# Loops in place of unrolled VectorE and ScalarE programs in a streamed LoRA-style matrix product

## The chip, the cores and the metric

One core of one Trainium2 chip. The metric is device microseconds of one execution, the median of several runs.

## The reference

```python
x_flat = x.reshape(-1, in_dim)            # 32768 x 256, fp32
y = x_flat @ W                            # W 256 x 256
lora_out = x_flat @ lora_A                # 256 x 16
lora_out = lora_out * lora_E              # 16
lora_out = lora_out @ lora_B              # 16 x 256
y = y + scale * lora_out                  # scale 1.0
return y.reshape(batch, seq_len, out_dim) # fp32
```

## The kernel before, in words

The kernel folds the low-rank branch into one weight: weff = W + (lora_A scaled by lora_E) @ lora_B, in bf16, made once at the start (lines 166 to 184). Then it streams x through: 33.5 MB in, 33.5 MB out.

The 32768 rows are cut by PLAN into five blocks of 56, 56, 48, 48 and 48 rows per partition. Three buffers of those sizes (SLOTS) hold blocks 0, 1 and 2; blocks 3 and 4 reuse the first two once the stores that read them have landed. Loads are cut into pieces (PIECES), each with a semaphore of its own; a store is one transfer for a whole block. The result of a row overwrites x in the same buffer. All loads of x, W and all stores are issued by SyncE (SP), so they run on one queue, in the order load 0, 1, 2, store 0, store 1, load 3, load 4, store 2, 3, 4. The three small matrices lora_A, lora_B and lora_E are issued by ScalarE on its own queue.

Computing goes in 32 steps of S = 8 rows per partition. In each step

- VectorE casts 8 rows to bf16 (`rounded`, L159, tile xb),
- TensorE transposes them, two bf16 values at a time packed as one fp32 word (`transposed`, L198, psum_xt),
- VectorE copies the transposed tile to SBUF (`copied`, L163, tile xt),
- TensorE multiplies by weff (`multiplied`, L209, psum_y), in two halves of G = 4 rows,
- ScalarE copies each half back into the block's buffer (L232, tile xy).

Everything is double-buffered by step parity. TensorE's program is already a loop (`Fori`) of two steps a turn, in the order transposes of step t+1, matmuls of step t. The programs of VectorE and ScalarE are written out step by step: each instruction waits for a semaphore to reach a count.

VectorE's order is rounded(0), rounded(1), then copied(t), rounded(t+2) for t = 0 to 31. At step 16 (HOLD) it stops until store 0 has landed and then makes five casts of 128x4096 into a tile nobody reads (L157); that is the pause that the title of the change speaks of. ISSUE_LOAD, ISSUE_STORE and ISSUE_PRODUCTS hold back certain issues of SyncE until so many transposes or products are done.

Of the kernel before, what the change touches and what calls it, by code (L numbers as in the profile page):

```python
# [4 lines left out]
PLAN = [56, 56, 48, 48, 48]  # L5

PIECES = {0: [16, 16, 24], 1: [16, 16, 24], 2: [24, 24], 3: [24, 24], 4: [24, 24]}

SLOTS = [56, 56, 48]
LEAD = 3  # L10
AFTER = {1: [3, 4]}

HOLD = 16, 0, 5


ISSUE_LOAD, ISSUE_STORE = {4: 20}, {3: 29}
ISSUE_PRODUCTS = {1: 30}

S, G = 8, 4
P = 128  # L20
FP32 = mybir.dt.float32
BF16 = mybir.dt.bfloat16
# [15 lines left out]
def kernel(tc, x, W, lora_A, lora_B, lora_E, scale, out):  # L38
    nc = tc.nc
    x_flat = x.flatten_outer_dims()  # L40
    out_flat = out.flatten_outer_dims()
    N, K = x_flat.shape
    M = out_flat.shape[1]
    R = lora_B.shape[0]
# [4 lines left out]
    steps = [(i, r) for i, b in enumerate(PLAN) for r in range(0, b, S)]  # L49
    NS = len(steps)  # L50
    assert NS % 2 == 0

    def rows_of(flat, i):
        b, r0 = PLAN[i], starts[i]
        return flat[r0:r0 + b * P, :].rearrange("(p b) k -> p b k", b=b)

    def sbuf(name, shape, dt):
        return nc.alloc_sbuf_tensor(name, shape, dt).ap()

    def psum(name, shape, dt):  # L60
        return nc.alloc_psum_tensor(name, shape, dt).ap()

    slots = [sbuf(f"xy{s}", [P, rows, K], FP32) for s, rows in enumerate(SLOTS)]
    a_sb = sbuf("a_sb", [P, KC, R], FP32)
    e_sb = sbuf("e_sb", [R, 1], FP32)
    w_sb = sbuf("w_sb", [P, KC, M], FP32)
    b_sb = sbuf("b_sb", [R, M], FP32)
    b_bf = sbuf("b_bf", [R, M], BF16)
    ate = sbuf("ate", [R, KC, P], BF16)
    weff = sbuf("weff", [P, KC, M], BF16)  # L70
    spare = sbuf("spare", [P, 2 * S, K], BF16)
    ident = sbuf("ident", [P, P], FP32)

    xb = [sbuf(f"xb{k}", [P, S, K], BF16) for k in range(2)]
    words = [t[:, :, :].rearrange("p s k -> p (s k)").bitcast(FP32).rearrange("p (s w) -> p s w", s=S) for t in xb]

    xt = [sbuf(f"xt{k}", [P, S, P], FP32) for k in range(2)]
    pairs = [t[:, :, :].rearrange("p s t -> p (s t)").bitcast(BF16).rearrange("p (s t c) -> p s t c", s=S, c=KC) for t in xt]
    ps_xt = [psum(f"psum_xt{k}", [P, S, P], FP32) for k in range(2)]
    ps_y = [psum(f"psum_y{k}", [P, G, M], FP32) for k in range(2)]  # L80
# [4 lines left out]
    s_w, s_a, s_b, s_e = (Count(nc, f"s_{k}") for k in "wabe")  # L85

    pieces = {}
    for i, b in enumerate(PLAN):
        parts = PIECES.get(i, [b])
        pieces[i] = [(sum(parts[:j]), n) for j, n in enumerate(parts)]  # L90
    s_ld = {(i, r): Count(nc, f"s_ld{i}_{r}") for i in pieces for r, n in pieces[i]}
    s_st = [Count(nc, f"s_st{i}") for i in range(len(PLAN))]
    s_id, s_set, s_v, s_t, s_m, s_y = (
        Count(nc, k) for k in ("s_id", "s_set", "s_v", "s_t", "s_m", "s_y"))
    tick = nc.alloc_semaphore("tick")


    can_m = nc.alloc_semaphore("can_m")
    can_t = [nc.alloc_semaphore(f"can_t{k}") for k in range(2)]
    can_y = [[nc.alloc_semaphore(f"can_y{h}_{k}") for k in range(2)] for h in range(S // G)]  # L100

    def slot(i):
        return slots[i % LEAD][:, :PLAN[i], :]

    opening = []

    def transfer(queue, count, **aps):
        ins = queue.dma_start(**aps)
        for names in opening:
            names.add(ins.ins.name)  # L110
        count.by(ins, 16)

    def load(i):
        for r, n in pieces[i]:
            transfer(nc.sync, s_ld[i, r], out=slot(i)[:, r:r + n, :], in_=rows_of(x_flat, i)[:, r:r + n, :])

    def store(i):
        transfer(nc.sync, s_st[i], out=rows_of(out_flat, i), in_=slot(i))

    def spent(engine, count):  # L120
        engine.wait_ge(count.sem, count.total).then_inc(count.sem, -count.total)

    def take(sem):
        nc.tensor.wait_ge(sem, 1).then_inc(sem, -1)
# [4 lines left out]
    transfer(nc.sync, s_w, out=w_sb, in_=W.rearrange("(p c) m -> p c m", c=KC))  # L129
    transfer(nc.scalar, s_a, out=a_sb, in_=lora_A.rearrange("(p c) r -> p c r", c=KC))  # L130
    transfer(nc.scalar, s_b, out=b_sb, in_=lora_B)
    transfer(nc.scalar, s_e, out=e_sb, in_=lora_E[:, None])
    load(0)
    opening.clear()
    tc.close()
# [1 line left out]
    for i in range(1, LEAD):  # L137
# [5 lines left out]
        out=ident, in_=ident, compare_op=mybir.AluOpType.not_equal, fill=1.0, base=0,  # L143
        pattern=[[-1, P]], channel_multiplier=1))


    def rounded(t):
        i, r = steps[t]
        if (i, r) in s_ld:
            nc.vector.wait_ge(s_ld[i, r].sem, 16)  # L150
        if t == HOLD[0]:

            for _ in range(10):
                nc.vector.engine_nop()
            nc.vector.wait_ge(s_st[HOLD[1]].sem, 16)
            for _ in range(HOLD[2]):
                nc.vector.tensor_copy(out=spare, in_=slot(i)[:, r:r + 2 * S, :]).then_inc(tick, 1)  # L157
                nc.vector.wait_ge(tick, 1).then_inc(tick, -1)
        nc.vector.tensor_copy(out=xb[t % 2], in_=slot(i)[:, r:r + S, :]).then_inc(can_t[t % 2], 1)  # L159

    def copied(t):
        nc.vector.wait_ge(s_t.sem, t + 1)
        nc.vector.tensor_copy(out=xt[t % 2], in_=ps_xt[t % 2]).then_inc(can_m, 1)  # L163


    nc.vector.wait_ge(s_b.sem, 16)
    s_v.by(nc.vector.tensor_copy(out=b_bf, in_=b_sb))  # L167
    nc.tensor.wait_ge(s_a.sem, 16)
    nc.tensor.wait_ge(s_id.sem, 2)
    for c in range(KC):  # L170
# [4 lines left out]
    s_v.by(nc.vector.tensor_scalar(  # L175
        out=ate, in0=ps_at, scalar1=e_sb, scalar2=float(scale),
        op0=mybir.AluOpType.mult, op1=mybir.AluOpType.mult))
    nc.tensor.wait_ge(s_v.sem, 2)
    for c in range(KC):
        aeb_done = nc.tensor.matmul(ps_aeb[:, c, :], ate[:, c, :], b_bf, start=True, stop=True)  # L180
    s_set.by(aeb_done)
    nc.vector.wait_ge(s_w.sem, 16)
    nc.vector.wait_ge(s_set.sem, 2)
    s_v.by(nc.vector.tensor_add(out=weff, in0=w_sb, in1=ps_aeb))  # L184
    rounded(0)
    rounded(1)
    for t in range(NS):
        copied(t)
        if t + 2 < NS:
            rounded(t + 2)  # L190

    nc.vector.sem_inc(can_t[NS % 2], 1)


    def transposed(k):
        nc.tensor.wait_ge(can_t[k], 1)
        for j in range(S):
            done = nc.tensor.transpose(ps_xt[k][:, j, :], words[k][:, j, :], ident)  # L198
            if j == 1:
                done.then_inc(can_t[k], -1)  # L200
        done.then_inc(s_t.sem, 1)

    def multiplied(k):
        take(can_m)
        for h in range(S // G):
            nc.tensor.wait_ge(can_y[h][k], 1)
            for j in range(G):
                for c in range(KC):
                    done = nc.tensor.matmul(  # L209
                        ps_y[h][:, j, :], pairs[k][:, h * G + j, :, c], weff[:, c, :],  # L210
                        start=(c == 0), stop=(c == KC - 1))
                if j == 0:
                    done.then_inc(can_y[h][k], -1)
            done.then_inc(s_m.sem, 1)

    transposed(0)
    nc.tensor.wait_ge(s_v.sem, 3)

    with nc.tensor.Fori(0, NS // 2):
        for k in range(2):  # L220
            transposed(1 - k)
            multiplied(k)
    s_t.total, s_m.total = NS + 1, NS * S // G

    for h in range(S // G):
        nc.scalar.sem_inc(can_y[h][0], 1)
    n = 0
    for i, r in [(i, r + g) for i, r in steps for g in range(0, S, G)]:
        n += 1
        nc.scalar.wait_ge(s_m.sem, n)  # L230
        t, h = divmod(n - 1, S // G)
        y = nc.scalar.copy(out=slot(i)[:, r:r + G, :], in_=ps_y[h])  # L232
        free = can_y[h][(t + 1) % 2]
        if r + G < PLAN[i]:
            y.then_inc(free, 1)
        else:
            done = s_y.by(y)
            if n < s_m.total:
                nc.scalar.wait_ge(s_y.sem, done)
                nc.scalar.sem_inc(free, 1)  # L240
            nc.sync.wait_ge(s_y.sem, done)
            if i in ISSUE_STORE:
                nc.sync.wait_ge(s_t.sem, ISSUE_STORE[i])
            if i in ISSUE_PRODUCTS:
                nc.sync.wait_ge(s_m.sem, ISSUE_PRODUCTS[i])
            store(i)
            for later in AFTER.get(i, []):
                nc.sync.wait_ge(s_st[later - LEAD].sem, 16)
                if later in ISSUE_LOAD:
                    nc.sync.wait_ge(s_t.sem, ISSUE_LOAD[later])  # L250
                load(later)


    for count in [s_a, s_id]:
        spent(nc.tensor, count)
    spent(nc.tensor, s_v)
    for count in [s_b, s_e, s_w, s_set] + list(s_ld.values()):
        spent(nc.vector, count)
    spent(nc.scalar, s_m)
    nc.tensor.wait_ge(can_y[0][NS % 2], 1).then_inc(can_y[0][NS % 2], -1)  # L260
    for count in [s_y, s_t] + s_st:
        spent(nc.sync, count)


# [33 lines left out]
```

## Time and profile before

| what | us |
|---|---|
| median of 3 runs (161.62 to 162.06) | 161.67 |
| the profiled execution's own time | 161.75 |
| its span, from the first instruction to the last | 160.4 |
| TensorE busy, matmuls | 91.8 (57%) |
| VectorE busy | 87.9 (55%) |
| ScalarE busy | 63.2 (39%) |
| GpSimd busy | 0.7 |
| 64 copies of ScalarE, L232, 1017 ns each | 61.9 |
| 512 matmuls, L209, 280 ns each | 63.7 |
| 264 transposes, L198, 287 ns each | 36.8 |
| 32 copies xt, L163, 1222 ns each | 39.1 |
| 32 casts xb, L159, 1220 ns each | 38.9 |
| 5 casts of the pause, L157, 2294 ns each | 11.5 |

Engines: PE is TensorE, PEld its weight loads, DVE VectorE, ACT ScalarE, POOL GpSimd, SP SyncE; SPq is SyncE's issue of transfers. The row of digits of an engine or of DMA cuts the span into 40 slices, each digit a busy share in tenths. DMA is the mean over the core's 16 DMA engines. Rows of stretches give, for each stretch of the span, its length, busy time and number of instructions of PE, PEld, DVE, ACT and POOL, the TensorE clock granted, the DMA share and the GB/s moved; packets are counted where they begin, so a share can pass 1. Rows of the timeline give start, duration, engine, line, operation and count. q1 is SyncE's queue, q10 ScalarE's, q14 the fetching of instructions.

### The profile page before, as it was taken

Reading aid. Unit: us, or ns where it says so; the run is one execution under the profiler, and the core shown is the slowest. Engines: PE = TensorE matmul, PEld = TensorE weight load, DVE = VectorE, ACT = ScalarE, POOL = GpSimd, SP = SyncE. Lnnn points to the kernel's source line nnn. Section 1 sums busy time; section 2 is a strip of 40 time slices with the busy share of each in tenths; the row PEclk is TensorE's granted clock in tenths of the full one; section 3 lists DMA queues with packets and bytes.
Section 4 is the critical chain, followed back from the end, with each engine's and each line's share of the span. In section 5 each row is a group of like instructions: output and inputs, shape, how many; then the busy total and the mean of one; then the engine's idle time right before and its main releaser. Section 6 shows DMA issues by size and latency. Waiting matters only on the chain. (4 is left out here: it accounts for less than half of the span.)

```text
span 160.4 us, 1883 instructions
## 1 busy us (share of the span) xinstructions
PE 91.8 (57%) x780; PEld 82.7 (52%) x780; DVE 87.9 (55%) x72; ACT 63.2 (39%) x65; POOL 0.7 (0%) x6
## 2 busy tenths in 40 slices
PE   0149999999999600000009999999999960000000
PEld 0028889999999500000008999999999950000000
DVE  0187769998988000039999669899898500000000
ACT  1100675868676700000001768686868670000000
POOL 1000000000000000000000000000000000000000
PEclk9999999999999975555555999999999999555555
DMA  5999999999999999999989999999999999999994
GB/s 179 409 433 447 429 415 433 449 435 411 466 404 392 458 457 457 457 443 457 415 386 382 423 404 460 411 455 423 496 404 404 466 453 429 404 417 490 429 429 196
DMA packets 2802, 67.42 MB, mean 420 GB/s; under 512 B 480, under 2 KB 496, under 8 KB 624
## 3 DMA queue, kind: packets, MB, share of 16 engines
q1 hardware_dynamic: 2592, 67.37, 98.0%
q10 hardware_dynamic: 208, 0.03, 0.2%
q14 instruction: 2, 0.02, 0.0%
HBM read 33.85 MB, written 33.55 MB: 420 GB/s over the span
## 5 line engine op out<-in xcount | busy, mean ns | idle before, releaser
L232 ACT COPY xy<-psum_y 128x1024 f32<-128x1024 f32 x64 | 61.9, 1017 | 65.5 <-PE psum_y L209 65.5
L209 PE MATMUL psum_y<-weff,xt 128*128 128x256 bf16 x512 | 63.7, 280 | 0.1
L209 PEld LDWEIGHTS psum_y<-weff,xt 128*128 128x128 bf16 x512 | 51.4, 101 | 7.1 <-issue 0.3
L198 PE MATMUL psum_xt<-ident,xb 128*128 128x128 f32 x264 | 36.8, 287 | 31.3 <-DVE xb L159 31.3
L198 PEld LDWEIGHTS psum_xt<-ident,xb 128*128 128x128 f32 x264 | 31.9, 148 | 32.7 <-DVE xb L159 32.3
L163 DVE COPY xt<-psum_xt 128x1024 f32<-128x1024 f32 x32 | 39.1, 1222 | 8.4 <-PE psum_xt L198 8.2
L159 DVE CAST xb<-xy 128x2048 bf16<-128x2048 f32 x32 | 38.9, 1220 | 3.7 <-DMA xy<-in_x_dram 3.4
L157 DVE CAST spare<-xy 128x4096 bf16<-128x4096 f32 x5 | 11.5, 2294 | 19.5 <-DMA out_dram<-xy 19.0
L167 DVE CAST b_bf<-b_sb 16x256 bf16<-16x256 f32 x1 | 0.3, 281 | 5.6 <-DMA b_sb<-in_lora_B_dram 5.6
L171 PE MATMUL psum_xt<-ident,a_sb 128*16 128x128 f32 x2 | 0.6, 396 | 4.2 <-POOL ident L142 4.2
L232 ACT ACT_TABLE_LOAD x1 | 1.3, 1283 | 3.5 <-PEq L136 3.5
L180 PE MATMUL psum_xt<-b_bf,ate 16*128 16x256 bf16 x2 | 0.6, 404 | 3.6 <-DVE ate L175 3.6
L171 PEld LDWEIGHTS psum_xt<-ident,a_sb 128*16 128x16 f32 x2 | 0.1, 90 | 4.2 <-DMA a_sb<-in_lora_A_dram 4.2
L180 PEld LDWEIGHTS psum_xt<-b_bf,ate 16*128 16x128 bf16 x2 | 0.1, 106 | 4.1 <-DVE ate L175 4.1
L175 DVE TENSOR_SCALAR ate<-psum_xt,e_sb 16x256 bf16<-16x256 f32 x1 | 0.5, 472 | 2.0 <-DMA e_sb<-in_lora_E_dram 2.0
L184 DVE TENSOR_TENSOR weff<-w_sb,psum_xt 128x512 bf16<-128x512 f32 x1 | 0.7, 689 | 0.8 <-PE psum_xt L180 0.8
L142 POOL TENSOR_SCALAR_AFFINE_SELECT ident<-ident 128x128 f32<-128x128 f32 x1 | 0.3, 294 | 0.2 <-POOL ident L140 0.2
L140 POOL MEMSET ident<- 128x128 f32 x1 | 0.2, 205 | 2.9 <-POOLq L136 2.9
L279 POOL MEMSET const-bfloat16-1.0<- 128x1 bf16 x1 | 0.1, 102 | 0.0
L279 POOL MEMSET const-uint8-127<- 128x1 uint8 x1 | 0.1, 102 | 0.0
L279 POOL MEMSET const-float32-0.0<- 128x1 f32 x1 | 0.1, 99 | 0.2 <-issue 0.2
L279 POOL MEMSET const-float32-1.0<- 128x1 f32 x1 | 0.1, 99 | 0.0
## 6 DMA issues: line engine op xcount, KB each, us to landing
xy<-in_x_dram SPq DMA_DIRECT2D x8, 3072.0 KB, 27.9
out_dram<-xy SPq DMA_DIRECT2D x3, 6144.0 KB, 28.2
out_dram<-xy SPq DMA_DIRECT2D x2, 7168.0 KB, 34.3
xy<-in_x_dram SPq DMA_DIRECT2D x4, 2048.0 KB, 17.8
w_sb<-in_W_dram SPq DMA_DIRECT2D x1, 256.0 KB, 3.0
a_sb<-in_lora_A_dram ACTq DMA_DIRECT2D x1, 16.0 KB, 3.1
b_sb<-in_lora_B_dram ACTq DMA_DIRECT2D x1, 16.0 KB, 4.4
e_sb<-in_lora_E_dram ACTq DMA_DIRECT2D x1, 0.1 KB, 6.2
```

Source lines behind the costliest of these rows:

```text
L142: s_id.by(nc.gpsimd.affine_select(out=ident, in_=ident, compare_op=mybir.AluOpType.not_equal, fill=1.0, base=0, pattern=[[-1, P]], channel ...
L157: nc.vector.tensor_copy(out=spare, in_=slot(i)[:, r:r + 2 * S, :]).then_inc(tick, 1)
L159: nc.vector.tensor_copy(out=xb[t % 2], in_=slot(i)[:, r:r + S, :]).then_inc(can_t[t % 2], 1)
L163: nc.vector.tensor_copy(out=xt[t % 2], in_=ps_xt[t % 2]).then_inc(can_m, 1)
L171: at_done = nc.tensor.transpose(ps_at[:, c, :], a_sb[:, c, :], ident)
L175: s_v.by(nc.vector.tensor_scalar(out=ate, in0=ps_at, scalar1=e_sb, scalar2=float(scale), op0=mybir.AluOpType.mult, op1=mybir.AluOpType.mult))
L180: aeb_done = nc.tensor.matmul(ps_aeb[:, c, :], ate[:, c, :], b_bf, start=True, stop=True)
L184: s_v.by(nc.vector.tensor_add(out=weff, in0=w_sb, in1=ps_aeb))
L198: done = nc.tensor.transpose(ps_xt[k][:, j, :], words[k][:, j, :], ident)
L209: done = nc.tensor.matmul(ps_y[h][:, j, :], pairs[k][:, h * G + j, :, c], weff[:, c, :], start=(c == 0), stop=(c == KC - 1))
L232: y = nc.scalar.copy(out=slot(i)[:, r:r + G, :], in_=ps_y[h])
L279: nc = _bacc.Bacc("TRN2", target_bir_lowering=False, num_devices=1)
```

## The change

- The three buffers become one tensor, xy, of RING = 160 rows; the blocks start in it at AT = 0, 56, 112, 0, 48.
- VectorE's program becomes two casts and two loops of two steps a turn (9 turns, then 7), ScalarE's two loops of two steps a turn (10, then 6). The row in the ring comes from the loop's register. Semaphores are counted down by the waiting instruction, so that each turn waits for the same value. The last copy of a turn signals through last_y, which ScalarE itself waits for before it frees the PSUM half and counts s_y, now once per two steps.
- GpSimd waits for each piece of x and adds its number of steps to s_rows; VectorE's casts wait for s_rows. The pause is on GpSimd, ahead of the piece that starts at step 17: it waits for store 0 and makes seven memsets of a 128x2048 fp32 tile, one after the other.
- SyncE's conditions for stores and loads are counts of s_y (turns).
- lora_E is issued by SyncE between W and the first piece of x. ScalarE copies it to a tile of its own (e_copy) before its loops.
- TensorE makes one matmul whose result nobody reads ahead of the product of lora_A and lora_B, and two behind it (`idle`).

```diff
-SLOTS = [56, 56, 48]
+RING, AT = 160, [0, 56, 112, 0, 48]
-HOLD = 16, 0, 5
-ISSUE_LOAD, ISSUE_STORE = {4: 20}, {3: 29}
-ISSUE_PRODUCTS = {1: 30}
+HOLD = 17, 0, 7
+ISSUE_LOAD, ISSUE_STORE = {4: 9}, {1: 8, 3: 14}
...
-    transfer(nc.scalar, s_e, out=e_sb, in_=lora_E[:, None])
+    transfer(nc.sync, s_e, out=e_sb, in_=lora_E[:, None])
...
+    t = 0
+    for i, r in s_ld:
+        n = sum(rows for first, rows in pieces[i] if first == r) // S
         if t == HOLD[0]:
-            for _ in range(10):
-                nc.vector.engine_nop()
-            nc.vector.wait_ge(s_st[HOLD[1]].sem, 16)
+            nc.gpsimd.wait_ge(s_st[HOLD[1]].sem, 16)
             for _ in range(HOLD[2]):
-                nc.vector.tensor_copy(out=spare, in_=slot(i)[:, r:r + 2 * S, :]).then_inc(tick, 1)
-                nc.vector.wait_ge(tick, 1).then_inc(tick, -1)
+                tick.by(nc.gpsimd.memset(spare, 0.0))
+                nc.gpsimd.wait_ge(tick.sem, tick.total)
+        nc.gpsimd.wait_ge(s_ld[i, r].sem, 16).then_inc(s_rows, n if t + n < NS else n + 2)
+        t += n
+
+    def idle(times):
+        for _ in range(times):
+            nc.tensor.matmul(ps_y[0][:, :2, :].rearrange("p g m -> p (g m)"), ident, w_sb[:, :, :].rearrange("p c m -> p (c m)"),
+                             start=True, stop=True)
...
+    nc.tensor.wait_ge(s_w.sem, 16)
+    idle(1)
     nc.tensor.wait_ge(s_v.sem, 2)
...
     s_set.by(aeb_done)
+    idle(2)
...
+    def rounded(k, first):
+        nc.vector.wait_ge(s_rows, 1).then_inc(s_rows, -1)
+        nc.vector.tensor_copy(out=xb[k], in_=xy[:, bass.ds(first, S), :]).then_inc(can_t[k], 1)
+
+    for k in range(2):
+        rounded(k, k * S)
+    around = RING // (2 * S) - 1
+    for turns, begin in ((around, 2 * S), (NS // 2 - around, 0)):
+        with nc.vector.Fori(0, turns) as turn:
+            for k in range(2):
+                nc.vector.wait_ge(s_t, 1).then_inc(s_t, -1)
+                nc.vector.tensor_copy(out=xt[k], in_=ps_xt[k]).then_inc(can_m, 1)
+                rounded(k, turn * (2 * S) + (begin + k * S))
...
+    nc.scalar.wait_ge(s_e.sem, 16)
+    nc.scalar.copy(out=e_copy, in_=e_sb)
...
+    for turns in (RING // (2 * S), NS // 2 - RING // (2 * S)):
+        with nc.scalar.Fori(0, turns) as turn:
+            for k in range(2):
+                for h in range(S // G):
+                    nc.scalar.wait_ge(s_m, 1).then_inc(s_m, -1)
+                    first = turn * (2 * S) + (k * S + h * G)
+                    y = nc.scalar.copy(out=xy[:, bass.ds(first, G), :], in_=ps_y[h])
+                    y.then_inc(can_y[h][1] if k == 0 else can_y[0][0] if h == 0 else last_y, 1)
+            nc.scalar.wait_ge(last_y, 1).then_inc(last_y, -1)
+            nc.scalar.sem_inc(can_y[1][0], 1)
+            nc.scalar.sem_inc(s_y.sem, 1)
+    s_y.total = NS // 2
+    rows = 0
+    for i, b in enumerate(PLAN):
+        rows += b
+        nc.sync.wait_ge(s_y.sem, -(-rows // (2 * S)))
+        if i in ISSUE_STORE:
+            nc.sync.wait_ge(s_y.sem, ISSUE_STORE[i])
+        store(i)
+        for later in AFTER.get(i, []):
+            nc.sync.wait_ge(s_st[later - LEAD].sem, 16)
+            if later in ISSUE_LOAD:
+                nc.sync.wait_ge(s_y.sem, ISSUE_LOAD[later])
+            load(later)
```

More of the change, by code (lines that the diff above doesn't have):

```diff
@@ L61, in psum @@
         return nc.alloc_psum_tensor(name, shape, dt).ap()
-    slots = [sbuf(f"xy{s}", [P, rows, K], FP32) for s, rows in enumerate(SLOTS)]
+    xy = sbuf("xy", [P, RING, K], FP32)
     a_sb = sbuf("a_sb", [P, KC, R], FP32)
     e_sb = sbuf("e_sb", [R, 1], FP32)
+    e_copy = sbuf("e_copy", [R, 1], FP32)
     w_sb = sbuf("w_sb", [P, KC, M], FP32)
@@ L70 @@
     weff = sbuf("weff", [P, KC, M], BF16)
-    spare = sbuf("spare", [P, 2 * S, K], BF16)
+    spare = sbuf("spare", [P, S, K], FP32)
     ident = sbuf("ident", [P, P], FP32)
@@ L92 @@
     s_st = [Count(nc, f"s_st{i}") for i in range(len(PLAN))]
-    s_id, s_set, s_v, s_t, s_m, s_y = (
-        Count(nc, k) for k in ("s_id", "s_set", "s_v", "s_t", "s_m", "s_y"))
-    tick = nc.alloc_semaphore("tick")
+    s_id, s_set, s_v, s_y, tick = (Count(nc, k) for k in ("s_id", "s_set", "s_v", "s_y", "tick"))
+    s_rows, s_t, s_m, last_y = (nc.alloc_semaphore(k) for k in ("s_rows", "s_t", "s_m", "last_y"))
     can_m = nc.alloc_semaphore("can_m")
@@ L102, in slot @@
     def slot(i):
-        return slots[i % LEAD][:, :PLAN[i], :]
+        return xy[:, AT[i]:AT[i] + PLAN[i], :]
     opening = []
@@ L144 @@
         pattern=[[-1, P]], channel_multiplier=1))
[L147 to L150, printed above, removed]
+    t = 0
+    for i, r in s_ld:
+        n = sum(rows for first, rows in pieces[i] if first == r) // S
         if t == HOLD[0]:
-            for _ in range(10):
-                nc.vector.engine_nop()
-            nc.vector.wait_ge(s_st[HOLD[1]].sem, 16)
+            nc.gpsimd.wait_ge(s_st[HOLD[1]].sem, 16)
             for _ in range(HOLD[2]):
-                nc.vector.tensor_copy(out=spare, in_=slot(i)[:, r:r + 2 * S, :]).then_inc(tick, 1)
-                nc.vector.wait_ge(tick, 1).then_inc(tick, -1)
[L159 to L163, printed above, removed]
+                tick.by(nc.gpsimd.memset(spare, 0.0))
[6 more added lines that the diff above has]
+                             start=True, stop=True)
     nc.vector.wait_ge(s_b.sem, 16)
@@ L184 @@
     s_v.by(nc.vector.tensor_add(out=weff, in0=w_sb, in1=ps_aeb))
[L185 to L192, printed above, removed]
+    def rounded(k, first):
[10 more added lines that the diff above has]
+                rounded(k, turn * (2 * S) + (begin + k * S))
     def transposed(k):
@@ L200, in transposed @@
                 done.then_inc(can_t[k], -1)
-        done.then_inc(s_t.sem, 1)
+        done.then_inc(s_t, 1)
     def multiplied(k):
@@ L213, in multiplied @@
                     done.then_inc(can_y[h][k], -1)
-            done.then_inc(s_m.sem, 1)
+            done.then_inc(s_m, 1)
     transposed(0)
@@ L222 @@
             multiplied(k)
-    s_t.total, s_m.total = NS + 1, NS * S // G
+    nc.scalar.wait_ge(s_e.sem, 16)
+    nc.scalar.copy(out=e_copy, in_=e_sb)
     for h in range(S // G):
         nc.scalar.sem_inc(can_y[h][0], 1)
[L227 to L251, printed above, removed]
@@ L254 @@
-    for count in [s_a, s_id]:
-        spent(nc.tensor, count)
[L256 to L261, printed above, removed]
+    for turns in (RING // (2 * S), NS // 2 - RING // (2 * S)):
[9 more added lines that the diff above has]
+            nc.scalar.sem_inc(s_y.sem, 1)
@@ new lines @@
+    s_y.total = NS // 2
[11 more added lines that the diff above has]
+            load(later)
+    for count in [s_a, s_id, s_v, s_b, s_e, s_w, s_set]:
+        spent(nc.tensor, count)
@@ L262 @@
+    for sem in [can_t[1]] + [can_y[h][0] for h in range(S // G)]:
+        take(sem)
+    nc.vector.wait_ge(s_t, 1).then_inc(s_t, -1)
+    for count in [s_y, tick] + list(s_ld.values()) + s_st:
         spent(nc.sync, count)
```

## The prediction

> **What bounds the kernel now.** I read the page's DMA rows first, because the busiest compute engine (TensorE, 57%) leaves nearly half of the span free.
>
> ```profile
> span 160.4 us, 1883 instructions
> PE   0149999999999600000009999999999960000000
> DMA  5999999999999999999989999999999999999994
> DMA packets 2802, 67.42 MB, mean 420 GB/s; under 512 B 480, under 2 KB 496, under 8 KB 624
> q1 hardware_dynamic: 2592, 67.37, 98.0%
> q14 instruction: 2, 0.02, 0.0%
> ```
>
> TensorE stands still for a quarter of the span in the middle and for a fifth at the end, while all 16 DMA engines stay at nine tenths or more between the first slice and the last. Then the stretches of the span, whose last column is what the DMA engines moved:
>
> ```profile
> 1.00:2.00 1.00, 0.00 (x0) 0.00 (x0) 0.00 (x0) 0.00 (x0) 0.00 (x0) 1.00 0.15 14
> 2.00:3.00 1.00, 0.00 (x0) 0.00 (x0) 0.00 (x0) 0.00 (x0) 0.00 (x0) 1.00 0.94 285
> 12.00:48.00 36.00, 35.87 (x305) 32.54 (x304) 30.74 (x28) 23.23 (x24) 0.00 (x0) 1.00 1.01 433
> 132.00:156.00 24.00, 0.00 (x0) 0.00 (x0) 0.00 (x0) 0.13 (x1) 0.00 (x0) 0.59 1.01 436
> 158.00:159.00 1.00, 0.00 (x0) 0.00 (x0) 0.00 (x0) 0.00 (x0) 0.00 (x0) 0.50 0.23 98
> ```
>
> The rate is 433 GB/s with every engine at work and 436 with none, so computing costs the transfers nothing. 67.42 MB at 434 GB/s is 155.3 us; the other 5.1 us of the span are the start (w_sb's first packet comes at 1.81 us), small packets and the switch from loads to stores, and the ragged end: by the packets' records the 16 engines finish between 158.7 and 160.0 us, 159.2 in the mean, and the last store's semaphore is complete at 160.41. So the time moves only if the first packets come later, a queue runs dry, or the last engine's lag changes. Last I took SyncE's issues and their landings, to see how long each transfer waits in the queue:
>
> ```profile
> 0.74 0.38 SPq L108 DMA_DIRECT2D w_sb<-in_W_dram  x1
> 1.17 4.61 SPq L108 DMA_DIRECT2D xy<-in_x_dram  x8
> 34.91 20.28 SPq L108 DMA_DIRECT2D out_dram<-xy  x2
> 70.61 25.51 SPq L108 DMA_DIRECT2D xy<-in_x_dram  x4
> 100.72 31.77 SPq L108 DMA_DIRECT2D out_dram<-xy  x3
> ```
>
> Everything runs in order on this one queue. Its contents land at: first eight loads 53.7 us, store 0 at 70.6, store 1 at 87.8, loads 3 and 4 at 102.4 and 117.0, stores 2, 3 and 4 at 131.5, 146.0 and 160.4. The issues came at 34.9 (store 0), 54.8 (store 1), 70.6 (load 3), 95.3 (load 4), 100.7, 118.9 and 132.2 (stores 2, 3, 4). Each is 7 us or more (load 4) and mostly 12 to 18 us before the work ahead of it ends. Those are the margins that the change must use up before it costs anything. The chain of waits (PE psum_y 19%, psum_xt 10%) ends at 132 us in store 4's issue, and is not the bound.
>
> **The change part by part.** The sum is made against the profiled execution: 161.75 us, of which 160.44 is span and 1.31 lies around it; it stands 0.08 above the median 161.67.
>
> *lora_E ahead of x on SyncE's queue.* An issue of this kind takes 0.38 to 0.45 us (e_sb's own was 0.44), so the first x piece is issued at about 1.61 instead of 1.17. Whether that shows depends on what runs then. w_sb's first packets began 0.69 to 1.0 us after its issue ended (1.12 to 1.81 and later), so x would be ready at 2.05 + 0.69 to 1.0 = 2.7 to 3.05 us. The engines are busy with w_sb and a_sb until 2.9 to 3.05 (one until 3.34), and the first x packet starts at 2.93. w_sb covers the delay but for 0 to 0.1 us. e_sb's own two packets per engine show 9 ns each, 0.02 us. Bounds: 0 (cover complete; perhaps a little below, since e_sb's 32 small packets no longer alternate with x) to 0.44 plus the 0.3 to 0.45 us that the first read of b_sb's rows held some engines (0.9). I take 0.07, near the row of w_sb, the transfer just ahead on the same queue. The Trainium skill, "DMA: Bandwidth & Descriptors", section "Specifications", gives about 0.6 us to the first byte on this path, less than this trace's 0.69 to 1.0 after the issue; by it x would be ready at 2.65 us and the term would be 0.02.
>
> *SyncE's later issues* (loads of x behind the barrier at line 136) move by the same 0.44 us; the queue then holds 16 us of loads, so nothing.
>
> *e_sb lands sooner* (3 queue places earlier than at 7.8 us), ate and weff follow some 2 us earlier, and three idle matmuls run in front. Each has 512 columns; the two 128-column ones of L171 took 0.59 us together, so four times 0.3 is 1.2 us, 3.6 for all, over by about 10.3 us. Step 0's cast needs the first x piece (landed 9.3) and 1.22 us, so its transposes start at 10.5 and are not pushed. The granted clock was 0.5 until 16.9 us, and that comes earlier now. It is worth up to 3 us to TensorE and nothing to the end: store 0 waits behind the loads until 53.7.
>
> *Store and load conditions.* Store 0 now needs 8 steps and store 1 needs 16, instead of 7 and 15 (two steps a turn): 2.62 us each (0.87 transposes, 1.75 matmuls), so about 37.5 and 58.5 us at the latest, 16 and 12 us before they are needed.
>
> *The pause.* Seven GpSimd memsets of 128x2048 take the place of five 2.29 us casts on VectorE. A memset takes 205 ns for 128 elements and 100 for one, 0.83 ns an element, so 1.80 us for 2048; with the 0.23 us between two dependent GpSimd instructions 2.03. Seven make 12.6 to 14.2 us, from 70.6 to 83.2 or 84.8 (before: 82.7). Seventeen steps go out ahead of it, and 16 instead of 15 are multiplied, as the matmuls of step t come behind the transposes of t+1. VectorE waits meanwhile for s_rows, and the cast of step 17 and all behind it wait with it, as they did behind the old pause.
>
> *After the pause.* From 84.8: cast 1.22, transposes 1.97 and matmuls 3.06 (the first after the old pause, clock 0.5) to 91.1, two more steps to 96.3. Step 20's cast needs load 3 (95.06), which brings the chain back to the old time: transposes to 97.2, matmuls to 98.9, 12 steps of 2.62 to 130.3, copies to 131.6. Store 4 is issued at 131.6 instead of 132.2, load 4 at about 95 (18 steps copied), store 2 at 100, store 3 at about 121 instead of 118.9; it is needed at 131.5.
>
> *The loops.* VectorE and ScalarE have register and branch instructions per turn that the trace of before doesn't show on them. Per step VectorE works 2.44 us and waits 0.26 for TensorE. Below: TensorE's own loop shows 0.1 us idle before 512 matmuls, so 0. Above: the longest gap called issue is 0.3 us; four a step give 2.44 + 1.2 = 3.64 us. The 12 steps behind 98.9 have until 144.9 for store 4 (its work ahead ends at 146.0, less w_sb's 1.07 to the first packet): (144.9 - 1.3 - 98.9) / 12 = 3.7 us a step. Even the upper bound is covered. Take 0.
>
> *Fewer instructions.* The two q14 packets (8 KB, at 86.5 and 104.5 us, 0.31 us each) should vanish with the unrolled programs. Each delayed one of 16 engines; following packet ends into starts, neither is on the two that finish last. Gain 0 to 0.31; I take 0.
>
> Sum: 161.75 + 0.07 = 161.82 for a profiled execution, 161.7 as a median.
>
> **The rivals.**
> 1. *Faster by the ragged end.* The last engine ends 0.8 us after the mean, and lags were made by the small packets of the first 5 us and the fetches, both of which change. If the lag halves or goes, and the first packets are no later, 161.0 to 161.3. Against: engines don't share out what one has left, so one late packet anywhere restores it.
> 2. *Slower by e_sb.* If x is ready only when e_sb has been read, the first x packet comes after 3.4 us instead of 2.93 and everything behind it moves: +0.5 to 0.9, 162.2 to 162.6. It decides from a bubble of 0.49 us. For it: x has only 0.35 us or so of cover. Against: e_sb's packets showed 9 ns.
> 3. *Slower by the loops.* If a step takes over 3.7 us, store 4 starts late: 12 times the excess, so +4 at 4.0 us and about 12 x 1.3 = 16 at a half clock for the whole second part (1.97 + 3.06 = 5.03 a step). A fetch behind the x packets could take as long as e_sb on the second queue, 6.2 us; once a loop is hidden by 13 us of margin, at each of 7 turns it gives 7 x 6.2 - 13 = 30 us more. The Trainium skill, "Runtime: NRT & Kernel Launch", section "Instruction fetch mechanics", says that a taken branch whose target is outside the fetched window stalls until it is fetched. TensorE's loop, with 0.1 us idle, shows no such stall.
>
> **How the numbers follow.** Forecast 0.48, rival 1 0.28, rival 2 0.16, rival 3 0.08. 0.3% is 0.49 us, about what a measurement of this kernel can tell from no change. Rival 1 ends partly inside it, the forecast's own tails (161.3 to 162.1) hardly leave it: faster 0.26, same 0.50, slower 0.24. The range goes from rival 1's 161.0 to the middle of rival 2, 162.5, and leaves out rival 3 and the edges.
>
> **What would show it.** Right: no idle DMA slice, the q1 row unchanged at 2592 packets or a few more, the first x packet before 3.1 us, store 4 issued before 145, q14 gone. Wrong: DMA slices under 9 in the middle, the 3 to 4 us stretch below 400 GB/s, VectorE steps over 3.7 us, or a last landing that moves without any of these.

## The result and the profile after

The changed kernel takes 163.44 us (median of 6 runs, 163.05 to 164.31) against 161.78 beside it: slower by 1.11%, ratio 1.0111 with a 95% interval of 1.0082 to 1.0141. The profiled execution took 163.25 us, of which 161.9 is span; 161.75 and 160.4 before. So 1.5 us more lie inside the span, and the 1.3 us around it are unchanged.

The page of the changed kernel, the rows that answer to those shown ahead of the change:

```profile
span 161.9 us, 2268 instructions
PE   0898869999999940000005999999999970000000
DMA  5999999999999999999996999999999999988991
DMA packets 2800, 67.41 MB, mean 416 GB/s; under 512 B 480, under 2 KB 496, under 8 KB 624
q1 hardware_dynamic: 2624, 67.37, 97.5%
...
L189 DVE CAST xb<-xy 128x2048 bf16 (+1 forms) x34 | 41.4, 1219 | 38.5 <-DVEq L188 38.4
...
L151 POOL MEMSET spare<- 128x2048 f32 x7 | 12.6, 1805 | 68.2 <-DMA out_dram<-xy 67.9
```

The bytes are the same, the two q14 packets (fetching of instructions) are gone, and q1 has 32 packets more, lora_E's 16 and as many semaphore writes. The DMA row shows a 6 in slice 22 and ends in 8, 8, 9, 9, 1, where the kernel before has an 8 in slice 21 and then nines up to a 4 in the last. These are not gaps. The row counts a packet's whole time in the slice in which it begins. With the packets' times split at the borders of the slices, every slice between the first and the last is full in both kernels, and only the last differs: 0.71 busy before, 0.47 now. There some engines have finished and others go on. SyncE's queue in the timeline (start, duration, count), and the stretches at the start and the end:

```profile
0.74 0.38 SPq L106 DMA_DIRECT2D w_sb<-in_W_dram  x1
1.17 0.42 SPq L106 DMA_DIRECT2D e_sb<-in_lora_E_dram  x1
1.65 4.42 SPq L106 DMA_DIRECT2D xy<-in_x_dram  x8
38.97 21.36 SPq L106 DMA_DIRECT2D out_dram<-xy  x2
72.36 25.30 SPq L106 DMA_DIRECT2D xy<-in_x_dram  x4
102.70 31.77 SPq L106 DMA_DIRECT2D out_dram<-xy  x3
```
```profile
2.00:3.00 1.00, 0.00 (x0) 0.00 (x0) 0.00 (x0) 0.00 (x0) 0.00 (x0) 1.00 1.06 296
3.00:4.00 1.00, 0.00 (x0) 0.00 (x0) 0.00 (x0) 0.20 (x1) 0.20 (x1) 1.00 0.87 249
158.00:159.00 1.00, 0.00 (x0) 0.00 (x0) 0.00 (x0) 0.00 (x0) 0.00 (x0) 0.50 0.11 49
159.00:160.00 1.00, 0.00 (x0) 0.00 (x0) 0.00 (x0) 0.00 (x0) 0.00 (x0) 0.50 0.35 148
```

x is issued at 1.65 us instead of 1.17. The packets that begin between 3 and 4 us carry only 249 GB/s (last column); the same row of the kernel before is

```profile
3.00:4.00 1.00, 0.00 (x0) 0.00 (x0) 0.00 (x0) 0.51 (x1) 0.43 (x2) 1.00 1.12 420
```

At the end packets still begin after 159 us (148 GB/s), where before there was nothing. And load 3, which is issued when store 0 has landed, comes at 72.36 instead of 70.61: 1.75 us have already been lost by then, no less than the 1.5 by which the span ends later.

Each transfer adds to its semaphore once per engine, so the trace has 16 landing times per transfer. They show what the sums over engines hide (us; first engine / median / last engine):

| kernel | first x piece | last load of blocks 0 to 2 | store 4 |
|---|---|---|---|
| before | 8.47 / 8.65 / 9.26 | 52.69 / 52.86 / 53.65 | 159.12 / 159.60 / 160.41 |
| changed | 8.55 / 8.83 / 10.09 | 53.01 / 53.21 / 55.42 | 159.48 / 159.78 / 161.88 |

The median engine is 0.2 us later. Three engines land the first x piece at 9.82, 9.93 and 10.09 us, and the rest by 8.97. The packet records, joined end to start, show the same from the first packet on: thirteen engines begin x at 2.93 to 3.28 us, three at 4.14 to 4.29. The three never catch up, and at the switch from loads to stores their lag grows once more: three load packets of 24 KB that start at 51.4 to 51.7 us take 2.38 to 2.48 us instead of 0.91, while the other engines already store.

### The profile page after: what moved, and what is told of

Read it like the earlier page. It is cut to its first block, busy times and chain, and to the rows that moved or that the text cites. A ratio compares the mean times of both kernels' runs of the same rounds, so it can differ in the third digit from the quotient of the medians.

```text
span 161.9 us, 2268 instructions
## 1 busy us (share of the span) xinstructions
PE 96.1 (59%) x786; PEld 82.6 (51%) x786; DVE 78.8 (49%) x69; ACT 63.3 (39%) x66; POOL 13.3 (8%) x13
## 3 DMA queue, kind: packets, MB, share of 16 engines
q1 hardware_dynamic: 2624, 67.37, 97.5%
## 5 line engine op out<-in xcount | busy, mean ns | idle before, releaser
L243 ACT COPY xy<-psum_y 128x1024 f32 x64 | 61.8, 1017 | 66.8 <-ACTq L241 66.8
L216 PE MATMUL psum_y<-weff,xt 128*128 128x256 bf16 x512 | 62.8, 277 | 0.8 <-PEq L122 0.4
L189 DVE CAST xb<-xy 128x2048 bf16 (+1 forms) x34 | 41.4, 1219 | 38.5 <-DVEq L188 38.4
L216 PEld LDWEIGHTS psum_y<-weff,xt 128*128 128x128 bf16 x512 | 50.7, 99 | 7.7 <-issue 1.6
L205 PE MATMUL psum_xt<-ident,xb 128*128 128x128 f32 x264 | 35.9, 281 | 31.1 <-DVE xb L189 31.0
L205 PEld LDWEIGHTS psum_xt<-ident,xb 128*128 128x128 f32 x264 | 30.8, 145 | 34.4 <-DVE xb L189 34.0
L151 POOL MEMSET spare<- 128x2048 f32 x7 | 12.6, 1805 | 68.2 <-DMA out_dram<-xy 67.9
L158 PE MATMUL psum_y<-w_sb,ident 128*128 128x512 f32 x6 | 5.7, 1085 | 0.0
L158 PEld LDWEIGHTS psum_y<-w_sb,ident 128*128 128x128 f32 x6 | 1.7, 326 | 1.5 <-issue 1.4
```

Of the source, the lines that this page charges most:

```text
L151: tick.by(nc.gpsimd.memset(spare, 0.0))
L158: nc.tensor.matmul(ps_y[0][:, :2, :].rearrange("p g m -> p (g m)"), ident, w_sb[:, :, :].rearrange("p c m -> p (c m)"), start=True, stop=True)
L189: nc.vector.tensor_copy(out=xb[k], in_=xy[:, bass.ds(first, S), :]).then_inc(can_t[k], 1)
L216: done = nc.tensor.matmul(ps_y[h][:, j, :], pairs[k][:, h * G + j, :, c], weff[:, c, :], start=(c == 0), stop=(c == KC - 1))
L243: y = nc.scalar.copy(out=xy[:, bass.ds(first, G), :], in_=ps_y[h])
```

## The experiments

Each time is compared with the kernel before, run beside it; the ratio is to that kernel, with a 95% interval in brackets. First x piece and last load are the landings on the first, the median and the last engine.

Theory A was: lora_E's transfer stands between W and x, so that x's first data come after W's transfer has run out; some engines start x about 1 us late and keep the lag. Theory B: the loops, the pause on GpSimd or the idle matmuls.

### lora_E back on ScalarE's queue

```diff
-    transfer(nc.sync, s_e, out=e_sb, in_=lora_E[:, None])
+    transfer(nc.scalar, s_e, out=e_sb, in_=lora_E[:, None])
```


> The changed kernel with lora_E back on ScalarE's queue, all else as changed. Theory A (lora_E ahead of x eats the cover that W's transfer gives the first x piece; three of sixteen DMA engines start about 1 us late, and the switch from loads to stores adds to their lag): about 161.8 us, last landing of the first x piece near 9.3 us instead of 10.1, of the last first-block load near 53.7 instead of 55.4. Theory B (the loops, the pause on GpSimd or the idle matmuls do it): about 163.4 us, the three late engines still there.

Measured: 162.27 us against 161.90 beside it, ratio 1.0018 (1.0006 to 1.0029). First x piece 8.48 / 8.61 / 8.76, last load 52.61 / 52.89 / 53.10. The late engines are gone, and 1.2 us with them. That is A, though 0.4 us stay that A had not asked for.

### lora_E alone moved, in the kernel before

```diff
-    transfer(nc.scalar, s_e, out=e_sb, in_=lora_E[:, None])
+    transfer(nc.sync, s_e, out=e_sb, in_=lora_E[:, None])
```


> The kernel before with lora_E alone moved to SyncE's queue ahead of x. Theory A: 163.0 to 163.8 us, with some engines landing the first x piece at about 10 us. Theory B: 161.7 to 162.1 us.

Measured: 163.72 us, ratio 1.0121 (1.0098 to 1.0144). One line gives the whole slowdown without any of the rest. First x piece 9.15 / 9.84 / 10.81: here nearly all engines are late. The stretches of this run at the start:

```profile
2.00:3.00 1.00, 0.00 (x0) 0.00 (x0) 0.00 (x0) 0.00 (x0) 0.00 (x0) 1.00 0.75 242
3.00:4.00 1.00, 0.00 (x0) 0.00 (x0) 0.00 (x0) 0.05 (x1) 0.20 (x1) 1.00 1.02 238
4.00:5.00 1.00, 0.33 (x2) 0.12 (x2) 0.28 (x1) 1.00 (x1) 0.30 (x2) 1.00 1.07 262
```

The DMA share says busy, but only 238 and 262 GB/s move: ten of the x packets that begin by 4.1 us last 1.3 to 1.9 us instead of 0.61. I read this as packets that have begun and wait for their data.

### lora_E on SyncE's queue, behind the first x piece

```diff
-    transfer(nc.sync, s_e, out=e_sb, in_=lora_E[:, None])
 ...
         for r, n in pieces[i]:
             transfer(nc.sync, s_ld[i, r], ...)
+            if (i, r) == (0, 0):
+                transfer(nc.sync, s_e, out=e_sb, in_=lora_E[:, None])
```


> The changed kernel with lora_E still on SyncE's queue, but behind the first piece of x instead of ahead of it. Theory A: about 161.8 us, since x is issued at 1.17 us again; ate and weff come later (lora_E lands behind the first piece, near 9 us) and this is hidden. Theory B, and also a theory that any lora_E transfer on this queue does it: about 163.4 us.

Measured: 162.33 us, ratio 1.0026 (1.0017 to 1.0036). The queue is the same and the transfer is the same; its place alone is worth 1.1 us.

```profile
1.17 0.42 SPq L106 DMA_DIRECT2D xy<-in_x_dram  x1
1.64 0.42 SPq L106 DMA_DIRECT2D e_sb<-in_lora_E_dram  x1
...
70.10 25.03 SPq L106 DMA_DIRECT2D xy<-in_x_dram  x4
```
```profile
3.00:4.00 1.00, 0.00 (x0) 0.00 (x0) 0.00 (x0) 0.19 (x1) 0.19 (x1) 1.00 1.20 489
```

x is back at 1.17 us, packets with 489 GB/s begin between 3 and 4 us, and load 3 is issued at 70.10. The first x piece lands at 8.28 / 8.48 / 8.57, on all engines within 0.3 us. lora_E lands near 8.7 us. The weight that needs it is made at 10.01 us instead of 7.60, and store 0 is issued no later for it (38.52 against 38.97).

### Without the idle matmuls

```diff
-    nc.tensor.wait_ge(s_w.sem, 16)
-    idle(1)
...
-    idle(2)
```


> The changed kernel without its three idle matmuls. Theory A: 163.4 us as changed, since TensorE is not on the path. Theory B in the form that the idle matmuls (their reads of w_sb, or the earlier full clock) disturb the first transfers: about 161.8 us.

Measured: 163.43 us, ratio 1.009 (1.0069 to 1.011), as the changed kernel. The idle matmuls neither cost nor bring anything. In the profiled execution seven engines begin x late, at 4.34 to 4.77 us, instead of three (first x piece 8.60 / 9.57 / 10.54). So the number of late engines is not fixed, though one trace of each kernel can't tell chance from the edit.

### lora_E ahead of W

```diff
+    transfer(nc.sync, s_e, out=e_sb, in_=lora_E[:, None])
     transfer(nc.sync, s_w, ...)
-    transfer(nc.sync, s_e, out=e_sb, in_=lora_E[:, None])
```


> The changed kernel with lora_E first on SyncE's queue, then W, then x. W and x are both issued 0.44 us later and W runs ahead of x again. Theory A: the whole stream moves by 0.44 us and no more, 162.3 + 0.4 = 162.7, and the first x piece lands on all engines within 0.5 us. Rival D (lora_E's small packets on the queue themselves hold engines for about 1 us, wherever ahead of x they stand): 163.4 or more.

Measured: 162.77 us, ratio 1.0053 (1.0039 to 1.0068): 0.44 us above the 162.33 with lora_E behind x, one issue's length. First x piece 8.79 / 9.05 / 9.55.

```profile
0.73 0.39 SPq L106 DMA_DIRECT2D e_sb<-in_lora_E_dram  x1
1.18 0.41 SPq L106 DMA_DIRECT2D w_sb<-in_W_dram  x1
1.64 4.51 SPq L106 DMA_DIRECT2D xy<-in_x_dram  x8
```

x is issued at 1.64 us, as in the changed kernel, but directly behind W, and the whole stream moves by one issue instead of some engines by 1 to 2 us. D is out.

### lora_B in lora_E's place

```diff
-    transfer(nc.scalar, s_b, out=b_sb, in_=lora_B)
-    transfer(nc.sync, s_e, out=e_sb, in_=lora_E[:, None])
+    transfer(nc.scalar, s_e, out=e_sb, in_=lora_E[:, None])
+    transfer(nc.sync, s_b, out=b_sb, in_=lora_B)
```


> The changed kernel with lora_E back on ScalarE's queue and lora_B (16 rows of 1 KB) in its place on SyncE's queue, between W and the first x piece. Theory A (any short transfer between W and x makes x late, whatever it carries): 163.0 to 163.8 with some engines about 1 us late at the first x piece. Rival D2 (it takes lora_E's four-byte pieces): 162.3.

Measured: 164.41 us (162.54 to 164.79), ratio 1.013 (1.009 to 1.017). First x piece 8.68 / 8.85 / 10.63, last load 52.87 / 53.29 / 55.71. It isn't the four-byte pieces: 16 rows of 1 KB do the same, and the median passes A's 163.8. Three engines are late again: they begin x at 4.03 to 4.23 us, the others by 3.62. The switch at 51 us adds its part (24 KB packets of 2.0 and 2.2 us). The last 0.8 us come later still. The last engine is 2.36 us behind the median at load 3 and 3.19 at the end, because here one late engine is also the one with the slow store packets that are described under theory O below. So the 1 us between this run and the changed kernel is not shown to come from the 16 KB. In this run 177 GB/s begin between 3 and 4 us:

```profile
3.00:4.00 1.00, 0.00 (x0) 0.00 (x0) 0.16 (x1) 0.20 (x1) 0.20 (x1) 1.00 0.70 177
```

### W twice ahead of x

```diff
+    transfer(nc.sync, s_again, out=w_again, in_=W.rearrange("(p c) m -> p c m", c=KC))
     load(0)
```
(and lora_E on ScalarE's queue)

> The changed kernel with lora_E on ScalarE's queue, and W loaded a second time, into a tile nobody reads, between W and the first x piece: 262 KB more, 0.6 us of all 16 engines at 434 GB/s. x is issued at 1.6 us as in the changed kernel. Theory A (what counts is whether the transfer ahead still runs when x's first data come; any transfer that is long enough covers a late issue): no late engines, about 162.3 + 0.6 = 162.9, faster than the changed kernel's 163.4 in spite of the added bytes. Rival C (the later issue of x by itself moves everything): 163.4 + 0.6 = 164.0.

Measured: 163.99 us, in two groups: four runs at 162.79 to 163.00 and six at 163.91 to 164.73. A's 162.9 is the first group. C's 164.0 is near the median, but not for C's reason: in the profiled execution, one of the second group, 15 engines land the first x piece at 8.94 to 9.30, where A puts them (8.48 + 0.6 = 9.1 for the median), and one at 11.60. Its first x packet begins at 5.33 us, the others' at 3.63 to 3.98, though the second W had landed on every engine by 4.39. So with a longer transfer ahead of x 15 engines are not late. For the one that is, the cover of such a transfer was not enough, and why isn't settled; nor is it known whether the other five long runs look the same.

### Theory O: a short pause, and the old schedule in the loops

What is left between the loops and the kernel before is 0.4 us (162.27 and 162.33 against 161.90). One engine has longer packets wherever computing runs beside a store: in the run with lora_E behind x, 48 KB packets at 115.9, 117.8, 119.8 ... 129.4 us take 0.11 to 0.14 us more than their 1.82, each starting where the one before ended, and the row ends when computing does. That engine ends last (160.97; the next one 159.65). The two runs of this section start from the kernel with lora_E behind x, and the edits are shown against that kernel.

```diff
-HOLD = 17, 0, 7
+HOLD = 17, 0, 1
```


> The kernel with lora_E behind the first x piece (162.3 us), with one memset in the pause instead of seven: computing starts again at about 72.4 us, runs some four steps beside store 1, and waits for load 3 at 95. Theory O (one of the 16 engines moves each store packet about 0.12 us slower while TensorE, VectorE and ScalarE work; that engine ends last, and 0.3 us more of this is what is left between the loops and the kernel before): about five more slow packets, +0.6 us, near 162.9. Rival: the slow engine has nothing to do with computing, 162.3.

Measured: 162.90 us, ratio 1.0063 (1.0052 to 1.0074). The time is O's. Five slow packets of 56 KB appear at 73.8, 76.0, 78.2, 80.4 and 82.7 us (0.05 to 0.13 us over their 2.12), beside store 1 where the other run had none, and the last engine ends 1.95 us behind the median instead of 1.60.

```diff
-PIECES = {..., 2: [24, 24], ...}
-HOLD = 17, 0, 7
-ISSUE_LOAD, ISSUE_STORE = {4: 9}, {1: 8, 3: 14}
+PIECES = {..., 2: [16, 32], ...}
+HOLD = 16, 0, 6
+ISSUE_LOAD, ISSUE_STORE = {4: 9}, {3: 14}
```


> The loops with lora_E behind the first x piece (162.3 us), and the pause put where it was before: ahead of step 16 instead of 17 (block 2's pieces are 16 and 32 rows for that), six memsets instead of seven, store 1 free after 14 steps. Computing ends about 2.6 us earlier ahead of the pause and 2 us earlier at the end, so some two or three packets of the slow engine fewer. Theory O (what is left between the loops and the kernel before is the longer overlap of computing with stores): 0.25 to 0.35 us less, 162.0, level with before within 0.1%. Rival L (loops or GpSimd's hand-out themselves cost 0.3 us): 162.3 as in the run without this.

Measured: 162.13 us against 161.84, ratio 1.0023 (1.0012 to 1.0034). 0.2 us less in the median than without it, but the ratios, 1.0023 and 1.0026, cannot be told apart, and the interval does not reach 1. In the profiled executions the extra time of the slow store packets adds up to 1.0 us in the kernel before, 1.4 with lora_E behind x, 1.9 with the short pause and 1.1 here. That is the order of the times, and speaks for O, from one trace each. How much of the rest belongs to the loops themselves stays open.

### The kernel before with lora_E behind the first x piece

The edit of the third experiment, in the kernel before.

> The kernel before with lora_E alone moved to SyncE's queue, behind the first x piece. Theory A: 161.7 to 161.9, no slower than before. If it is faster than before by 0.3 us or more, the small packets on the second queue cost the kernel before something too.

Measured: 161.82 us beside 161.82, ratio 0.9979 (0.995 to 1.0009). No slower, and not clearly faster: the first x piece is more even (8.27 / 8.48 / 8.62), yet the last engine ends 1.22 us behind the median, and the one with the slow store packets ends last but one. No run clearly beat the kernel before.

## Why the prediction was wrong

*The step that failed is "lora_E ahead of x on SyncE's queue".* I sized it at 0.07 us; it measures 1.1 us in the loops (163.44 against 162.33) and 1.8 in the kernel before (163.72 against 161.90). Three things in it were wrong.

First, when x is ready. I took it from W's row, 0.69 to 1.0 us after the issue ends. x's issue ended at 2.06 us. On thirteen engines the first x packet ends between 3.54 and 4.36; at 0.61 us for an unhindered packet the data were ready at 2.93 to 3.75, an estimate of 0.9 to 1.7 us after the issue. The other three engines begin at 4.14 to 4.29, 2.1 to 2.2 us after it. In the kernel before this didn't show, since x was issued 0.48 us sooner and the packets stood behind W until 2.9 us. The cover that I put at 0.35 us was too thin for such a spread. The Trainium skill's 0.6 us to the first byte ("DMA: Bandwidth & Descriptors", "Specifications") is further off still here; the measurement decides.

The later issue and the lost cover are not the whole account. With x issued at 1.64 us directly behind W, all 16 engines begin it by 3.73 us (lora_E ahead of W), and 15 by 3.98 with W twice (the sixteenth at 5.33). With a short transfer directly ahead of x, and x issued at the same time to 0.01 us, some begin only after 4.0: three in the changed kernel, seven without the idle matmuls, three with lora_B, three in the kernel before with lora_E alone moved. This points to the short transfer itself making x later on some engines, from one trace each. How it would do that no run shows.

Second, I took a delay as one number for all 16 engines. It falls on some of them by 1 us or more and on the others hardly at all, and the last engine sets the end. My rival 1 argued from just this ragged end, but only for a gain.

Third, what comes later. I had no term for the switch from loads to stores. There the late engines lose another 0.6 to 1.0 us where one or three are late (last engine minus median: 1.26 to 2.21 in the changed kernel, 1.78 to 2.42 with lora_B, 2.45 to 3.11 with W twice), 0.4 us where seven are (0.97 to 1.38, no idle matmuls), and nothing in the run in which most engines were late (0.97 to 1.00). That the other engines' stores do it is what the times suggest; no run tested it.

*Rival 2*, with a chance of 0.16, had the right transfer and the right direction, and in part the mechanism. The sign set down against the forecast, a 3 to 4 us stretch below 400 GB/s, came: it is 249. But rival 2 had the first x packet after 3.4 us and everything behind it moved; the first one still begins at 2.93, and only three engines come after 4. Its price of 0.5 to 0.9 us was for all engines alike, so the measured 1.66 us lies outside it and outside the range. All the signs listed for the forecast came true too (first x packet before 3.1 us, 2624 packets on q1, store 4 before 145, no q14). They did not test the step that failed. (The 6 in the DMA row is not the idle slice that was listed against it.)

*Computing and transfers.* The forecast read from 433 against 436 GB/s that computing costs the transfers nothing. For the mean rate that holds. It does not hold for the engine with the slow store packets, which ends last in the loops with lora_E on ScalarE's queue or behind x (1.4 us behind the median and more).

*The loops.* The steps held: 2.62 us a step as before, and store 4 is issued at 134.1 us (131.6 forecast) against a need near 146. Rival 3 is out. ScalarE's copies are unchanged at 1017 ns, and no fetch shows on q14 in the span: the stall of a branch to code that isn't there ("Runtime: NRT & Kernel Launch" of the Trainium skill, "Instruction fetch mechanics") doesn't show in these loops. A small rest of 0.2 to 0.3% remains in the changed kernel without the late engines, against the 0 that I took; theory O would account for some of it.

*The pause* was sized right: a memset takes 1.805 us (1.80 forecast), seven with their waits 12.98 us:

```profile
72.39 12.98 POOL L151 MEMSET spare<- 128x2048 f32 x7 [67.86 <-DMA out_dram<-xy]
```

*Idle matmuls*: they take 5.7 us instead of 3.6 and end at 11.2, not 10.3. They cost nothing, as forecast, since what TensorE does at the start bounds nothing. The granted clock of 0.5 until 16.9 us, which the forecast names there, stands in no row: the stretches say 1.00, and the clock's records begin only at 16.95 us (11.06 now). What the rows show is a slow start, 3.68 us for the first 16 transposes, against 2.23 behind the idle matmuls.

*Fewer instructions*: the two q14 packets vanished and gained nothing that could be measured, as I took it.

## What to carry to other kernels

In a kernel that one saturated DMA queue bounds, the place of a small transfer in the issue order can cost far more than its bytes: put it behind the first large load, not between the transfer that covers the start and the load that it covers. Read the 16 landing times of a transfer one by one, not their mean: the last engine sets the end, and in these runs a lag of 1 us from the first microseconds lasted to the end. A cover is worth only what it has to spare, and the latency of the transfer behind it should be taken from where it stood uncovered, not from another transfer's row.

## What the runs showed of the hardware that was not expected

- A 64-byte transfer in the issue order made a kernel of 162 us 1.1 us (loops) to 1.8 us (unrolled) slower; 16 KB in the same place made the loops 2.1 us slower (164.41 against 162.27), of which some 0.8 us, in the profiled execution, came from the slow store packets falling on a late engine.
- The lag is uneven: 3 engines of 16 in one profiled execution, 7 in another of nearly the same kernel, almost all in a third (the unrolled kernel with lora_E moved), by about 1 us each.
- At the first switch from loads to stores all runs but one lose 0.5 to 0.9 us per engine in the mean (the packets' time above the usual, added up), in load packets of 24 KB that last up to 2.5 us instead of 0.91 (32 KB and 1.2 us in the run with the old schedule); in the run in which nearly all engines were late it was 0.2 us.
- In every profiled execution one engine of 16 takes about 0.1 us more for a store packet of 48 KB while the compute engines work, about 1 us in all, and is among the last four to end. Which partitions it serves, and what on the compute side does it, was not tried.
